# Late modulation columns loaded two ahead, and the last features' products put at the end, in a fused two-block kernel

## The chip, the cores and the metric

The kernel runs on one core of a Trainium2 chip. The metric is the device time of one execution in microseconds (us). A core has TensorE (PE, with its weight loads PEld), VectorE (DVE), ScalarE (ACT), GpSimd (POOL) and SyncE (SP), whose queue issues nearly all DMAs here.

## The reference

Two transformer-like blocks on 256 tokens of 1024 features, in float32. Only block 1 and the end of block 2's mixing touch the change.

```
mod = silu(c) @ w_ada + b_ada            # six vectors of 1024: shift1, scale1, gate1, shift2, scale2, gate2
h   = rmsnorm(x, norm1_g) * (1 + scale1) + shift1
qa, ka, va, qi, ki, wi, qb, kb, vb, ga, gb = split(h @ w_in)
ya  = sparse_attention(qa, ka, va, index scores of qi, ki, wi: the 64 best keys)
yb  = stick_breaking_attention(qb, kb, vb)
m   = sigmoid(ga) * (ya @ w_proj_a) + sigmoid(gb) * (yb @ w_proj_b)
x   = x + gate1 * (m @ w_out)
h2  = rmsnorm(x, norm2_g) * (1 + scale2) + shift2
x   = x + gate2 * experts(h2)            # 16384 experts, the longest part by far
x   = block2(x)                          # SSM and mLSTM branches, mixed @ w_out_2, again experts
```

## The kernel before

Activations stand transposed, features on partitions, 256 tokens along the free side. Every matrix that is streamed comes in column tiles of 128 x 1024 floats (512 KB), one DMA each on SP's queue (`wload`, L200). A tile in `raw` is split in two fp32r parts: `whi` by a cast on ScalarE (L180) and `wlo` = raw - whi on VectorE (L181). The stream has 3 `raw`, 3 `whi` and 2 `wlo` buffers. `flow` (L208) loads one tile ahead of the one that it hands out.

One output tile is 24 products into one PSUM tile (`wstat`, L217): for each of 8 feature groups k, whi·hi and whi·lo, and after these 16 the 8 of wlo·hi. PSUM has four tiles "mm" and four "acc".

Block 1 in order: `w_vab` and `w_qk` together with the first 16 modulation dots; then 30 tiles of `w_in`, numbered 0 to 29 here, through `proj` (L483): 6 for the index vectors, 8 for qa and ka, 16 for the two gates. Between them run generators by budget (`Side.run`): stick-breaking (`stick`), index scores and the choice of keys (`index`), attention (`attend`, which reads `toep`, the table of position biases). Then the mixing stage (L700): 8 tiles of `w_pab`, the products ya·w_proj_a and yb·w_proj_b, gated and added on VectorE (L711 to L713) and split into `mhi`, `mlo`. Then 8 tiles of `w_out` (L723), whose results go into `xT` (L727), into two scaled parts `u` for the queries (`unscaled`, L302) and into a row sum of squares on TensorE (`sq_acc`, L275). `queries` (L309) makes the first 5 query tiles from u, and the reciprocal root of the row sum scales them afterwards.

The late modulation vectors (indices 2, 3 and 4: gate1, shift2, scale2) are 24 dots (`mod_dot`, L343), each the product of a 128 x 1024 piece of `w_mod` with the row `crow`, summed along the row, one VectorE instruction and a short read of the accumulator. Its 512 KB come by a DMA from the same SP queue. `mods_late` (L356) is a generator: a step loads a piece into one of 2 buffers and computes its dot. `proj` gives it 1.3 in each of the first 14 tiles and 0.35 in the rest, the mixing stage 0.8 a tile; a step costs 1.3 and is taken while the sum is positive. `late.finish()` after the mixing stage runs what is left.

What the code says is a program order with priorities. The framework's scheduler orders the instructions of each engine at build time from that, from dependences and from an estimated timeline, so products of two tiles can stand between each other. `issue_after(x)` keeps an instruction behind x on its engine.

Block 2 has the same shape at its end: mixing, 8 tiles of `w_out_2` (L1496) and `queries`.

Of the kernel before, what the change touches and what calls it, by code (L numbers as in the profile page):

```python
# [9 lines left out]
F32 = mybir.dt.float32  # L10
# [11 lines left out]
P = 128  # L22
T = 256
D = 1024
NK = 8
# [84 lines left out]
class K:  # L110
# [106 lines left out]
    def wstat(self, p, w, a, n, k0=0, ks=None, parts=(0, 1), first=True, last=True):  # L217
# [6 lines left out]
        for c, (x, y, k) in enumerate(ops):  # L224
            nc.tensor.matmul(p, x[:, (k0 + k) * P:(k0 + k + 1) * P], y[:, k, :], start=first and c == 0,  # L225
                             stop=last and c == len(ops) - 1)

    def wmove(self, acc, w, a, k, n, t0=0):

        nc = self.nc  # L230
        whi, wlo = w
        ahi, alo = a
        for tt in range(2):
            ts = slice(t0 + tt * P, t0 + (tt + 1) * P)
            for i, (x, y) in enumerate(((ahi, whi), (ahi, wlo), (alo, whi))):
                for h in range(2):
                    nc.tensor.matmul(acc[2 * tt + h], x[:, k, ts], y[:, h * 512:(h + 1) * 512],  # L237
                                     start=k == 0 and i == 0, stop=k == n - 1 and i == 2)
# [70 lines left out]
    def queries(self, flow, u, x, a, b, pss, pool, tags):  # L309


        nc, NU = self.nc, self.NU
        n = T if b is None else T + 2
        room = [self.t(self.const, [P, D], F32, "row", 2).rearrange("p (i t) -> p i t", t=T)
                for _ in range(0, NU, 4)]
        qb = None if b is None else self.t(pool, [P, NU], F32, "qb")
        self.qs = []
        h2 = self.act_pair()
        at = 0
        for i in range(NU):  # L320
            w = next(flow)
            p = self.ps()
            if i == 0:
                self.wstat(p[:, :n], w, u, NK, parts=(0,), last=False)
                self.sq_acc(pool, pss, x[:, NK - 1], NK - 1, tags[0])
                r = self.rstd_t(pool, pss, tags[1])
                self.wstat(p[:, :n], w, u, NK, parts=(1,), first=False)
            else:
                self.wstat(p[:, :n], w, u, NK)
            q = room[i // 4][:, i % 4]  # L330
            nc.vector.tensor_tensor(q, p[:, :T], r, ALU.mult)
            if b is not None:
                nc.scalar.copy(qb[:, i:i + 1], p[:, T:T + 1])
                nc.scalar.activation(q, q, AF.Identity, bias=qb[:, i:i + 1])
            self.qs.append((i, q))
            e = min(NK, 2 * (i + 1))
            self.scaled(pool, x, r, a, b, *h2, tag=tags[2], ks=range(at, e))
            at = e
        self.w0 = next(flow)
        return h2  # L340


    def mod_dot(self, i, k, raw):  # L343

        self.nc.sync.dma_start(raw, self.A["w_mod"][i, k])
        self.nc.vector.scalar_tensor_tensor(raw, raw, 1.0, self.crow, op0=ALU.mult, op1=ALU.mult,
                                            accum_out=self.mods[:, i, k:k + 1])

# [6 lines left out]

    def mods_late(self, pool, parts):  # L356

        for i in parts:
            for k in range(NK):
                raw = self.t(pool, [P, D], F32, "raw", 2)  # L360
                with self.tc.issue_after(self.wdma.ins):
                    self.mod_dot(i, k, raw)
                yield 1.3
            self.mod_end(i, 0, NK, "norm2_g" if i == 4 else None)

    def mod_gate2(self, pool):

# [23 lines left out]
    def block1(self):  # L391
        nc, A, tc = self.nc, self.A, self.tc
        v = nc.vector
        es = ExitStack()
        with es:
            wk = self.sub(es, "b1")
# [5 lines left out]
            for i in range(2):  # L402
                x = self.t(self.const, [P, D], F32, f"x{i}")
# [5 lines left out]
            for i in range(2):  # L409
                p = self.ps("acc")  # L410
# [27 lines left out]
            for k in range(0, NK, 2):  # L438
                p = self.ps()
# [10 lines left out]
            with tc.tile_pool(name="mods", bufs=1, side="right", reuse_waits="tile") as mp:  # L450
                for k in range(NK):
                    for i in (1, 0):
                        self.mod_dot(i, k, self.t(mp, [P, D], F32, "raw", 4))
                    a, b = (self.mods[:, i, k:k + 1] for i in (1, 0))
                    nc.scalar.activation(a, a, AF.Identity, scale=self.col("norm1_g", k), bias=gb[:, k:k + 1])
                    nc.scalar.activation(b, b, AF.Identity, bias=self.col("b_ada", k))
                    w = self.wload(A["w_vab"][k])
                    f = self.t(wk, [P, T], F32, "hnf", 2)
                    nc.scalar.activation(f, xr[:, k], AF.Identity, scale=a, bias=b)
                    self.split(h[0][:, k], h[1][:, k], f)  # L460
                    self.wmove(acc, w, h, k, NK)
                    whi, wlo = self.wload(A["w_qk"][k])
                    for i, (x, y) in enumerate(((whi, h[0]), (whi, h[1]), (wlo, h[0]))):
                        for j in range(8):
                            nc.tensor.matmul(pqk[j // 2][:, j % 2 * T:(j % 2 + 1) * T], x[:, j * P:(j + 1) * P], y[:, k],  # L465
                                             start=k + i + j % 2 == 0, stop=k == NK - 1 and i == 2 and j % 2 == 1,
                                             skip_group_check=True)
# [7 lines left out]
            for i in range(4):  # L475
                nc.scalar.activation(qkb[:, 2 * i:2 * i + 2], pqk[i].rearrange("p (k t) -> p k t", k=2), AF.Copy,
                                     scale=0.125 if i < 2 else 1.0)
            late = Side(self.mods_late(wk, (2, 3, 4)))
            budget = iter([1.3] * 14)
            flow = self.flow(*(A["w_in"][i] for i in range(30)), *(A["w_pab"][i] for i in range(NK)),  # L480
                             *(A["w_out"][i] for i in range(NK)), *(A["wq1"][i] for i in range(self.NU + 1)))

            def proj(dst, n=P, scale=None):  # L483
                w = next(flow)
                p = self.ps()
                self.wstat(p[:, :T], w, h, NK)
                late.run(next(budget, self.bl))
                if scale:
                    nc.scalar.activation(dst, p[:n, :T], AF.Copy, scale=scale)
                else:  # L490
                    nc.scalar.copy(dst, p[:n, :T])
# [183 lines left out]
            for i in range(8):  # L675
                if i < 4:
                    proj(qa[:, i], scale=0.125)
                else:
                    proj(ka[:, i - 4])
                if i % 2 == 0:  # L680
                    with tc.issue_after(self.wdma.ins):
                        nc.sync.dma_start(toep[:, i:i + 2], A["toep"][:, i:i + 2])
                ix.run(2.4)
                side.run(0.8)
            ix.finish()
# [11 lines left out]
            last = self.last  # L697
            mhi = self.t(wk, [P, NK, T], F32R, "qkb")
            mlo = self.t(wk2, [P, NK, T], F32R, "m_lo")
            for c in range(NK):  # L700
                w = next(flow)
                late.run(self.bs)
                pa = self.ps()
                self.wstat(pa[:, :T], w, ya, 4)
                pb = self.ps()
                self.wstat(pb[:, :T], w, yb, 4, k0=4)
                with tc.issue_after(last.ins):
                    last = nc.scalar.activation(sg[:, c:16:8], sg[:, c:16:8], AF.Sigmoid)
                m1 = self.t(wk2, [P, T], F32, "m1", 2)
                m2 = self.t(wk2, [P, T], F32, "m2", 2)  # L710
                nc.vector.tensor_tensor(m1, pa[:, :T], sg[:, c], ALU.mult)  # L711
                nc.vector.tensor_tensor(m2, pb[:, :T], sg[:, 8 + c], ALU.mult)
                nc.vector.tensor_tensor(m1, m1, m2, ALU.add)  # L713
                self.split(mhi[:, c], mlo[:, c], m1)
            self.ln_exp(last)
            late.finish()
            pss = self.ps("acc")
            u = self.t(wk2, [P, 2, NK, T + 2], F32R, "sg")
            u = (u[:, 0], u[:, 1])
            a2, b2 = self.mods[:, 4], self.mods[:, 3]  # L720
            bb = b2.unsqueeze(2).to_broadcast([P, NK, 2])
            self.split(u[0][:, :, T:], u[1][:, :, T:], bb)
            for c in range(NK):  # L723
                w = next(flow)
                p = self.ps()
                self.wstat(p[:, :T], w, (mhi, mlo), NK)
                nc.vector.scalar_tensor_tensor(xT[:, c], p[:, :T], self.mods[:, 2, c:c + 1], xT[:, c],  # L727
                                               op0=ALU.mult, op1=ALU.add)
                self.unscaled(u, xT, a2, c)
                if c < NK - 1:  # L730
                    self.sq_acc(wk, pss, xT[:, c], c)
# [693 lines left out]
    wait, bt = 3, 0.9  # L1425
    NU = 5
    ha, hi = 100, 100
    bl, bs, b5, bm, bf = 0.35, 0.8, 1.3, 1.8, 1.1

    def mix(self, wk, es, xm, M, sz, sgs, sgm, ysg):  # L1430

# [64 lines left out]
        for c in range(NK):  # L1496
            w = next(flow)
            p = self.ps()
            self.wstat(p[:, :T], w, (mx[0][:, :, :T], mx[1][:, :, :T]), NK)
            v.tensor_tensor(x3T[:, c], p[:, :T], x3T[:, c], ALU.add)  # L1500
            self.unscaled(u, x3T, g2, c)
            if c > 0:
                self.sq_acc(wk, pss, x3T[:, c - 1], c - 1, "cs")
# [500 lines left out]
```

## Time and profile before

| | |
|---|---|
| median of three executions | 2151.61 us (2148.75 to 2153.57) |
| profiled execution | 2151.88 us |
| its span, first to last instruction | 2150.2 us |
| TensorE busy | 2116.2 us (98%) |
| VectorE busy | 1615.7 us (75%) |
| ScalarE busy | 1118.5 us (52%) |
| TensorE's mean granted clock | 0.994 |
| DMA, mean over the span | 187 GB/s |

Busy time counts an engine's instructions from start to end. TensorE's instructions overlap one another, so its busy share says when it had something to do, and the granted clock how fast it was allowed to. Times in the trace count from the start of the span.

### The profile page before, as it was taken

How to read it: one execution, taken by the hardware profiler on the slowest of the kernel's cores; microseconds unless marked ns; L12 is line 12 of the kernel's file. 1: busy time of each engine (PE TensorE's matmuls, PEld its weight loads, DVE VectorE, ACT ScalarE, POOL GpSimd, SP SyncE). 2: the span in 40 equal slices, each digit the busy share in tenths (PEclk: the TensorE clock that was granted, in tenths of full speed). 3: DMA queues.
4: the chain of work that ended last, by engine and by line, in shares of the span. 5: the costliest groups of instructions: out<-in, count | busy, mean ns of one | idle time of the engine just before them, and what ended most of it. 6: DMA issues, size and time to landing. Idle time of an engine off the chain costs nothing.

```text
span 2150.2 us, 39275 instructions
## 1 busy us (share of the span) xinstructions
PE 2116.2 (98%) x14926; PEld 1925.0 (90%) x14926; DVE 1615.7 (75%) x3728; ACT 1118.5 (52%) x2157; POOL 20.8 (1%) x71
## 2 busy tenths in 40 slices
PE   8999999999999999999999999999999999999998
PEld 7889999999999887777788989999999998888886
DVE  8687799778889698666566457899688896555565
ACT  6546555455444554555464565455555445445553
POOL 0100000000000000000000000000000000000000
PEclk9999999999999999999999999999999999999999
DMA  9755556655555777767666525566555556666664
GB/s 333 248 191 180 177 170 195 186 167 161 164 164 162 249 227 238 203 202 205 197 187 191 184 79 157 181 183 196 167 158 165 161 166 187 194 196 192 192 193 138
DMA packets 127472, 402.44 MB, mean 187 GB/s; under 512 B 19617, under 2 KB 31521, under 8 KB 127026
## 3 DMA queue, kind: packets, MB, share of 16 engines
q1 hardware_dynamic: 127282, 399.93, 60.9%
q8 instruction: 117, 1.92, 0.4%
q14 instruction: 73, 0.60, 0.1%
HBM read 389.75 MB, written 9.03 MB: 185 GB/s over the span
## 4 chain that ended last, share of the span: by engine, by line
PE 90%; DMA 4%; DVE 3%; ACT 2%; issue 1%; POOL 0%; SPq 0%; DVEq 0%; ACTq 0%; POOLq 0%
PE ps_mm L225 47%; PE ps_acc L1126 31%; PE ps_acc L1015 1%; PE ps_acc L1016 1%; DVE wlo L181 1%; ACT whi L180 1%; PE ps_acc L237 1%; PE ps_mm L465 1%; DMA raw<-in_wq 1%; DMA raw<-in_v 1%; DMA raw<-in_w_in 1%; PE ps_acc L878 1%; PE ps_mm L243 1%; PE ps_mm L1367 1%; PE ps_acc L1662 0%
## 5 line engine op out<-in xcount | busy, mean ns | idle before, releaser
L180 ACT CAST whi<-raw 128x1024 fp32r<-128x1024 f32 x628 | 660.5, 1052 | 788.7 <-PE ps_acc L1126 279.4
L181 DVE TENSOR_TENSOR wlo<-raw,whi 128x1024 fp32r<-128x1024 f32 x521 | 637.0, 1223 | 319.4 <-ACT whi L180 180.9
L225 PE MATMUL ps_mm<-act_hi,whi 128*128 128x256 f32 (+1 forms) x2608 | 651.2, 288 | 3.7 <-ACT whi L180 1.2
L225 PE MATMUL ps_mm<-act_lo,whi 128*128 128x256 f32 (+1 forms) x2608 | 637.7, 283 | 0.0
L225 PEld LDWEIGHTS ps_mm<-act_hi,whi 128*128 128x128 f32 x2608 | 490.4, 189 | 9.7 <-issue 3.4
L225 PEld LDWEIGHTS ps_mm<-act_lo,whi 128*128 128x128 f32 x2608 | 492.2, 189 | 2.6 <-issue 1.9
L225 PE MATMUL ps_mm<-act_hi,wlo 128*128 128x256 f32 (+1 forms) x2544 | 354.8, 281 | 0.0
L225 PEld LDWEIGHTS ps_mm<-act_hi,wlo 128*128 128x128 f32 x2544 | 324.5, 189 | 1.4 <-issue 1.0
L181 DVE TENSOR_TENSOR xwlo<-raw,whi 128x1024 fp32r<-128x1024 f32 x107 | 130.8, 1222 | 82.8 <-ACT whi L180 81.4
L1126 PE MATMUL ps_acc<-whi,gh 128*128 128x512 f32 x328 | 103.4, 396 | 0.1
L1126 PE MATMUL ps_acc<-whi,gl 128*128 128x512 f32 x328 | 103.2, 396 | 0.1
L1126 PE MATMUL ps_acc<-whi,clo 128*128 128x512 f32 x328 | 102.6, 394 | 0.1
L1126 PE MATMUL ps_acc<-wlo,I1T 128*128 128x512 f32 x328 | 100.9, 390 | 0.0
L1126 PE MATMUL ps_acc<-whi,chi 128*128 128x512 f32 x328 | 89.0, 390 | 0.8 <-ACT chi L180 0.8
L1126 PE MATMUL ps_acc<-whi,I2T 128*128 128x512 f32 x328 | 88.5, 390 | 0.8 <-ACT I2T L180 0.8
L1126 PE MATMUL ps_acc<-whi,I1T 128*128 128x512 f32 x328 | 88.5, 390 | 0.0
L1126 PEld LDWEIGHTS ps_acc<-whi,chi 128*128 128x128 f32 x328 | 61.5, 188 | 14.1 <-ACT chi L180 1.2
L1126 PEld LDWEIGHTS ps_acc<-whi,I2T 128*128 128x128 f32 x328 | 61.4, 188 | 14.0 <-ACT I2T L180 1.2
L1126 PEld LDWEIGHTS ps_acc<-whi,gh 128*128 128x128 f32 x328 | 60.3, 188 | 14.6 <-issue 2.0
L1126 PEld LDWEIGHTS ps_acc<-wlo,I1T 128*128 128x128 f32 x328 | 61.6, 188 | 13.1
L1126 PEld LDWEIGHTS ps_acc<-whi,I1T 128*128 128x128 f32 x328 | 61.3, 188 | 13.0 <-ACT I1T L180 0.3
L1126 PEld LDWEIGHTS ps_acc<-whi,clo 128*128 128x128 f32 x328 | 60.6, 188 | 13.8 <-issue 1.2
(585 smaller groups left out, 3383.3 us busy)
## 6 DMA issues: line engine op xcount, KB each, us to landing
raw<-in_u SPq DMA_DIRECT2D x256, 512.0 KB, 3.7
raw<-in_v SPq DMA_DIRECT2D x256, 512.0 KB, 4.3
raw<-in_w_in SPq DMA_DIRECT2D x66, 512.0 KB, 4.3
raw<-in_w_mod SPq DMA_DIRECT2D x40, 512.0 KB, 5.3
raw<-in_wq SPq DMA_DIRECT2D x32, 512.0 KB, 3.8
raw<-in_w_out SPq DMA_DIRECT2D x16, 512.0 KB, 3.7
raw<-in_w_vab SPq DMA_DIRECT2D x8, 512.0 KB, 5.3
raw<-in_w_qk SPq DMA_DIRECT2D x8, 512.0 KB, 5.3
```

The source lines that it names most:

```text
L180: nc.scalar.copy(hi, src)
L181: nc.vector.tensor_tensor(lo, src, hi.bitcast(F32), ALU.subtract)
L225: nc.tensor.matmul(p, x[:, (k0 + k) * P:(k0 + k + 1) * P], y[:, k, :], start=first and c == 0, stop=last and c == len(ops) - 1)
L237: nc.tensor.matmul(acc[2 * tt + h], x[:, k, ts], y[:, h * 512:(h + 1) * 512], start=k == 0 and i == 0, stop=k == n - 1 and i == 2)
L243: self.nc.tensor.transpose(out, in_, self.ident[b:b + n, b:b + n])
L465: nc.tensor.matmul(pqk[j // 2][:, j % 2 * T:(j % 2 + 1) * T], x[:, j * P:(j + 1) * P], y[:, k], start=k + i + j % 2 == 0, stop=k == NK - 1 ...
L878: nc.tensor.matmul(p2[:, tt * P:(tt + 1) * P], q[:, tt * P:(tt + 1) * P], keys[:, hc // 8, (hc % 8) * P:(hc % 8 + 1) * P], start=tt == 0, ...
L1015: nc.tensor.matmul(o, oa[:, i], ob[:, i], start=i == 0, stop=False, skip_group_check=True)
L1016: nc.tensor.matmul(o, oa[:, i], oc[:, i], start=False, stop=i == 3, skip_group_check=True)
L1126: nc.tensor.matmul(acc[2 * tt + lo // 512][:, lo % 512:(hi - 1) % 512 + 1], x[:, ts], y[:, lo:hi], start=i == 0 and q == 0, stop=i == P - ...
L1367: nc.tensor.matmul(p[:64, i * P:(i + 1) * P], bbz[:, r, i].rearrange("p e c -> p (e c)"), ca[:, r, i, 0:8].rearrange("p l c -> p (l c)"), ...
```

## The change

The late dots get three buffers, and a step first issues the loads of the pieces up to two ahead, then computes its own dot. Their order becomes 2, 4, 3. The budget is 1.3 in the first 6 w_in tiles, 0.65 in the next 8 and 0.57 in the last 16; the mixing stage has none, and the first 7 w_out tiles have 1.3 each, the eighth what is left. The columns that carry shift2 into the queries are written in the eighth w_out tile. The four loads of `toep` move from w_in tiles 6, 8, 10 and 12 to 10, 11, 12 and 13. `wlast` gives one tile's products in the order of the features: both parts of groups 0 to 6, then both parts of group 7. The first `w_out` tile, the first `w_out_2` tile and the first query tile use it; in the query tile the last row sum stands between the two and the reciprocal root behind both.

```diff
+    def wlast(self, p, w, a, between=None):
+
+        self.wstat(p, w, a, NK, ks=range(NK - 1), last=False)
+        if between:
+            between()
+        self.wstat(p, w, a, NK, ks=(NK - 1,), first=False)
+
...
             if i == 0:
-                self.wstat(p[:, :n], w, u, NK, parts=(0,), last=False)
-                self.sq_acc(pool, pss, x[:, NK - 1], NK - 1, tags[0])
+                self.wlast(p[:, :n], w, u, lambda: self.sq_acc(pool, pss, x[:, NK - 1], NK - 1, tags[0]))
                 r = self.rstd_t(pool, pss, tags[1])
-                self.wstat(p[:, :n], w, u, NK, parts=(1,), first=False)
...
     def mod_dot(self, i, k, raw):
 
-        self.nc.sync.dma_start(raw, self.A["w_mod"][i, k])
...
-        for i in parts:
-            for k in range(NK):
-                raw = self.t(pool, [P, D], F32, "raw", 2)
+        todo = [(i, k) for i in parts for k in range(NK)]
+        raws = []
+        for n, (i, k) in enumerate(todo):
+            for j in range(len(raws), min(n + 3, len(todo))):
+                raws.append(self.t(pool, [P, D], F32, "raw", 3))
                 with self.tc.issue_after(self.wdma.ins):
-                    self.mod_dot(i, k, raw)
-                yield 1.3
-            self.mod_end(i, 0, NK, "norm2_g" if i == 4 else None)
+                    self.nc.sync.dma_start(raws[j], self.A["w_mod"][todo[j]])
+            self.mod_dot(i, k, raws[n])
+            yield 1.3
+            if k == NK - 1:
+                self.mod_end(i, 0, NK, "norm2_g" if i == 4 else None)
...
-            late = Side(self.mods_late(wk, (2, 3, 4)))
-            budget = iter([1.3] * 14)
+            late = Side(self.mods_late(wk, (2, 4, 3)))
+
+            budget = iter([1.3] * 6 + [0.65] * 8 + [0.57] * 16)
...
-                late.run(next(budget, self.bl))
+                late.run(next(budget))
...
-                if i % 2 == 0:
+                if i > 3:
                     with tc.issue_after(self.wdma.ins):
-                        nc.sync.dma_start(toep[:, i:i + 2], A["toep"][:, i:i + 2])
+                        nc.sync.dma_start(toep[:, 2 * i - 8:2 * i - 6], A["toep"][:, 2 * i - 8:2 * i - 6])
...
             for c in range(NK):
                 w = next(flow)
-                late.run(self.bs)
                 pa = self.ps()
...
-            late.finish()
...
-            self.split(u[0][:, :, T:], u[1][:, :, T:], bb)
             for c in range(NK):
                 w = next(flow)
+                if c < NK - 1:
+                    late.run(1.3)
+                else:
+                    late.finish()
+                    self.split(u[0][:, :, T:], u[1][:, :, T:], bb)
                 p = self.ps()
-                self.wstat(p[:, :T], w, (mhi, mlo), NK)
+                if c == 0:
+                    self.wlast(p[:, :T], w, (mhi, mlo))
+                else:
+                    self.wstat(p[:, :T], w, (mhi, mlo), NK)
...
-            self.wstat(p[:, :T], w, (mx[0][:, :, :T], mx[1][:, :, :T]), NK)
+            mix = (mx[0][:, :, :T], mx[1][:, :, :T])
+            if c == 0:
+                self.wlast(p[:, :T], w, mix)
+            else:
+                self.wstat(p[:, :T], w, mix, NK)
```

## Rows read from the trace of the kernel before

**Rows 1.** The page, busy time, share of the span and instructions of each engine.

```profile
PE 2116.2 (98%) x14926; PEld 1925.0 (90%) x14926; DVE 1615.7 (75%) x3728; ACT 1118.5 (52%) x2157; POOL 20.8 (1%) x71
```

**Rows 2.** Windows: length, busy PE, PEld, DVE, ACT, POOL, clock, DMA share, GB/s.

```profile
62.00:82.00 20.00, 20.00 (x163) 18.59 (x162) 13.23 (x20) 10.39 (x18) 2.52 (x4) 1.00 0.86 307
82.00:110.00 28.00, 24.36 (x135) 18.96 (x135) 18.90 (x36) 12.52 (x30) 5.71 (x8) 0.82 0.50 185
110.00:143.00 33.00, 32.67 (x244) 28.77 (x244) 29.45 (x80) 14.68 (x30) 2.60 (x6) 1.00 0.50 161
143.00:197.00 54.00, 52.53 (x413) 47.22 (x412) 39.07 (x82) 34.63 (x77) 1.46 (x2) 1.00 0.56 188
197.00:224.00 27.00, 24.24 (x194) 23.13 (x194) 23.99 (x43) 14.54 (x21) 0.00 (x0) 1.00 0.73 262
224.00:228.00 4.00, 4.00 (x22) 4.00 (x22) 3.86 (x11) 1.96 (x4) 0.00 (x0) 0.57 0.46 137
228.00:252.00 24.00, 24.00 (x194) 23.68 (x193) 15.21 (x25) 13.43 (x23) 0.00 (x0) 1.00 0.53 154
```

**Rows 3.** Waits of TensorE, 197 to 300: total us, times, longest.

```profile
PE ps_mm L225 <- DVE m L711: 2.6, 1, 2.6
PE ps_mm L225 <- ACT qb L333: 0.6, 1, 0.6
```

**Rows 4.** Windows of L346 alone (busy DVE, two instructions a dot), clock, DMA, GB/s.

```profile
197.00:228.00 31.00, 6.14 (x10) 0.94 0.70 246
```

**Rows 5.** Waits of TensorE, 62 to 110.

```profile
PE ps_mm L586 <- ACT relu L592: 2.6, 2, 1.4
PE ps_acc L533 <- POOL sp L528: 1.1, 1, 1.1
```

**Rows 6.** Waits of VectorE, 62 to 110.

```profile
DVE raw L346 <- DMA raw<-in_w_mod: 9.4, 8, 2.4
```

**Rows 7.** Timeline of VectorE: start, duration, instruction, idle time before it.

```profile
82.17 1.23 DVE L346 SCALAR_TENSOR_TENSOR raw<-raw,crow 128x1024 f32<-128x1024 f32 x1 [2.43 <-DMA raw<-in_w_mod]
83.33 0.08 DVE L346 DVE_READ_ACCUMULATOR raw<-raw,crow 128x1 f32 x1
```

**Rows 8.** Timeline of SP's issues.

```profile
77.55 0.42 SPq L345 DMA_DIRECT2D raw<-in_w_mod  x1
78.01 0.43 SPq L682 DMA_DIRECT2D toep<-in_toep  x1
86.92 0.33 SPq L204 DMA_DIRECT2D raw<-in_w_in  x1
...
90.60 0.33 SPq L204 DMA_DIRECT2D raw<-in_w_in  x1
...
97.28 0.33 SPq L345 DMA_DIRECT2D raw<-in_w_mod  x1
```

**Rows 9.** Timeline of ScalarE.

```profile
94.80 1.04 ACT L180 CAST whi<-raw 128x1024 fp32r<-128x1024 f32 x1 [2.38 <-DMA raw<-in_w_in]
```

**Rows 10.** Groups of VectorE, 197 to 226: count, busy us, mean ns, idle before.

```profile
L181 DVE TENSOR_TENSOR wlo<-raw,whi 128x1024 fp32r<-128x1024 f32 x9 | 10.9, 1219 | 0.3 <-ACT whi L180 0.3
...
L711 DVE TENSOR_TENSOR m<-ps_mm,sg 128x256 f32<-128x256 f32 x7 | 2.9, 418 | 0.5 <-PE ps_mm L225 0.5
```

**Rows 11.** Timeline of TensorE in w_out.

```profile
237.63 0.59 PE L279 MATMUL ps_acc<-sq,ones 128*128 128x256 f32 x2
...
238.18 1.12 PE L225 MATMUL ps_mm<-qkb,wlo 128*128 128x256 f32 x8
239.14 0.28 PE L225 MATMUL ps_mm<-qkb,whi 128*128 128x256 f32 x1
```

**Rows 12.** Groups of VectorE, 228 to 252.

```profile
L727 DVE SCALAR_TENSOR_TENSOR xT<-ps_mm,mods,xT 128x256 f32<-128x256 f32 x7 | 3.4, 483 | 7.2 <-PE ps_mm L225 7.2
L306 DVE SCALAR_TENSOR_TENSOR sg<-xT,mods,sg 128x256 fp32r<-128x256 f32 x7 | 3.3, 481 | 0.4 <-ACT sg L305 0.4
```

**Rows 13.** The page, DMA issues: KB each, median us from issue to landing.

```profile
raw<-in_w_mod SPq DMA_DIRECT2D x40, 512.0 KB, 5.3
```

More of the change, by code (lines that the diff above doesn't have):

```diff
@@ L452, in block1 @@
                     for i in (1, 0):
-                        self.mod_dot(i, k, self.t(mp, [P, D], F32, "raw", 4))
+                        raw = self.t(mp, [P, D], F32, "raw", 4)
+                        nc.sync.dma_start(raw, A["w_mod"][i, k])
+                        self.mod_dot(i, k, raw)
                     a, b = (self.mods[:, i, k:k + 1] for i in (1, 0))
@@ L1427 @@
     ha, hi = 100, 100
-    bl, bs, b5, bm, bf = 0.35, 0.8, 1.3, 1.8, 1.1
+    b5, bm, bf = 1.3, 1.8, 1.1
     def mix(self, wk, es, xm, M, sz, sgs, sgm, ysg):
```

## The prediction

> **What bounds the kernel now.** I read the page first. TensorE is busy for 98% of the span and no other engine comes near it [rows 1], so a change in block 1 can only pay where TensorE stands idle or runs at its half clock. The view by windows shows where that is in the stretches that this change touches [rows 2]. Three stretches have neither idle time nor a low clock (62 to 82, 228 to 252) or almost none (110 to 143). Two are poor:
>
> - 82 to 110 (w_in tiles 8 to 12, stick-breaking and index work between them): busy 24.36 of 28.00 us, so 3.64 idle, at a granted clock of 0.82. The clock has two levels, 2.4 and 1.2 GHz; a mean of 0.82 is 0.36 of 28 us = 10.1 us at the lower one, in which half the work is lost: 5.0 us. Together 8.7 us.
> - 197 to 228 (mixing stage, start of w_out): 2.76 us idle in 197 to 224, then a clock of 0.57 over 4.00 us, 1.7 us lost. Together 4.5 us.
>
> 143 to 197 adds 1.47 us of idle time. So what this change can reach in block 1 is about 8.7 + 4.5 + 1.5 = 14.7 us.
>
> Then I asked who is late. In 197 to 228 it is one wait of 2.6 us: the next product needs a PSUM tile that VectorE (L711) has not read yet [rows 3]. VectorE is busy 23.99 of 27.00 us there [rows 2], of which 6.1 us are five modulation dots at L346 [rows 4]; the sixth of that region stands ahead of 197. VectorE is the bound of the mixing stage, TensorE should be next.
>
> In 82 to 110 the waits are small ones on ScalarE's relu and GpSimd's mask [rows 5], and the cause lies further back. VectorE waited 9.4 us in 62 to 110 for w_mod loads, eight times [rows 6]. Its queue is in order: the dot at 82.17 came 2.43 us late [rows 7], and behind it stood the stick work and the weight splits that free stream buffers. So SP, whose last issues were at 77.55 and 78.01, loaded no weights until 86.92 [rows 8]. Then everything started at once: four w_in, four w_mod and two toep loads from 86.92 to 97.28. The w_in load of 90.60 was the one ScalarE waited for until 94.80 (2.38 us idle) [rows 8, 9], the relu of the index work stood behind that cast, TensorE idled, and its clock fell.
>
> **The change, part by part.** All in microseconds against the profiled execution, 2151.88 (span 2150.2 and 1.7 around it; 0.3 above the median of 2151.61).
>
> *How many dots go where.* From the budgets, one dot costing 1.3 and a step taken while the debt is positive. Before: 14 in tiles 0 to 13, 4 in tiles 14 to 29, 6 in the mixing stage or at its end. After: 6 in tiles 0 to 5, 4 in tiles 6 to 13, 8 in tiles 14 to 29, none in the mixing stage, 6 in the first six w_out tiles. The number of dots by then is the same, 18. Loads run two ahead: 12 instead of 14 by tile 13, and 4 fall into w_out.
>
> *Mixing stage.* Six dots of 1.22 leave it (7.3). Per tile VectorE then has one split at 1.22 and four operations at 0.42 (L711 and three like it), 2.9 as durations [rows 10], and less on the clock, since each overlaps the next (the dot of 82.17 took 1.23, its successor started 1.16 later [rows 7]). TensorE has 24 products at 0.12 = 2.9 (eight from 238.18 to 239.14 [rows 11]). The 2.8 of idle time and the 1.7 of clock both go: **-4.5**. Bounds 0 (if another chain takes the wait) and -4.5.
>
> *Tiles 6 to 13.* Four dots instead of eight, no dot waits for its own load, and the first toep pair moves from tile 6 to tile 10, the others to 11, 12 and 13. In the burst of 86.92 to 97.28, two w_mod and one or two toep loads go away, some 1.6 of 5.0 MB. The 2.43 wait at the head of the chain goes. What is late next is the chain VectorE, ScalarE, GpSimd, TensorE of the stick work itself. I take somewhat over half of 8.7: **-5.0**. Bounds 0 and -8.7.
>
> *Tiles 14 to 29.* Four dots more (4.9 on VectorE, which goes from 39.07 to 44 of 54 busy), four loads more (2.1 MB on 188 GB/s over 54 us, 227). VectorE in 110 to 143, at 29.45 of 33, gets lighter, and the late weight of 143 to 149 with it. **-0.5**; bounds -1.5 and +1.5, the idle time of that stretch gone or doubled.
>
> *w_out, first six tiles.* VectorE has a split, xT and the low half per tile, 1.22 + 0.48 + 0.48 [rows 10, 12], and now a dot: 3.4 as durations, some 3.1 as they overlap. TensorE has 2.9 of products and 0.4 of the fp32 row sum (237.63 to 238.18, less one product [rows 11]), 3.3. VectorE goes from 15.21 to about 22.5 of 24 [rows 2]. What hides the dots is that margin of 0.2 a tile, and it is thin. **+1.0**; bounds 0 and +3 (about the one wait of 2.6 that a full VectorE cost in the mixing stage [rows 3]).
>
> *First step.* Three w_mod loads stand ahead of w_in tile 2, where one did. Two more 0.5 MB loads at 307 GB/s are 3.4 us for that one weight. TensorE has no idle time in 62 to 82 to show how near the weights are; the two tiles that are already loaded (5.7 us of products) hide it. **0**; bound +1.7 if only half is hidden.
>
> *Last features last* (the first w_out tile, the first w_out_2 tile, and the first query tile, whose code both blocks run). Feature 7 is needed after 21 products instead of 14, that is 0.8 later. But the waits of TensorE have none at any of them (the longest in 197 to 300 are those of [rows 3]): the build's scheduler already puts the second tile's products between those of the first. So nothing to gain, bound -0.2. In the query tile the row sum now comes after 21 instead of 16 products, so the reciprocal root is up to 0.6 later; TensorE waits 0.6 for a query copy (L333) in block 1 [rows 3], which can grow. **+0.3**; bounds 0 and +1.2, 0.6 in each block.
>
> Sum: -4.5 - 5.0 - 0.5 + 1.0 + 0 + 0.3 = -8.7, so 2151.9 - 8.7 = **2143.2**.
>
> The idle rows and the clock rows were added above since TensorE's busy time alone would show 3.64 lost in 82 to 110. The Trainium skill (Perfetto Trace Analysis, Identifying the Most-Contended Engine) says that matmul occupancy misleads and that the busy share of weight loads is the better measure. By it 82 to 110 has lost 28.00 - 18.96 = 9.0, which agrees with the 8.7 [rows 2]; but 110 to 143 and 143 to 197 would then have lost 4.2 and 6.8 where the idle rows show 0.3 and 1.5. That reading is the first rival.
>
> **The rivals.**
>
> *More comes back.* Weight loads leave 11.0 unfilled in 110 to 197 [rows 2]. If steadier weights filled half of it, 5.5 more: 2137.7. Against it: TensorE hardly waits there, and the index and attention products are small or fp32 and leave the loader idle by their form. 0.05.
>
> *Only the mixing stage gains.* The early stretch may stay as it is: its waits end on relu and on GpSimd [rows 5], and the scheduler orders all engines anew at build. Then -4.5 - 0.5 + 1.0 + 0.3 = -3.7: 2148.2. For it: the same amount of w_mod by tile 13 less two. Against: the 2.43 wait ahead of the empty load queue. 0.15.
>
> *The mixing stall moves to w_out.* VectorE at its limit there gives back 4.5 where I have 1.0 in mind: -8.7 + 3.5 + 1.0 for a product that waits for a split = -4.2: 2147.7. 0.13.
>
> *Slower: dots in w_out wait for their loads.* This is one mechanism, at VectorE's queue in the first six w_out tiles. A dot that waits there as the longest did (2.4 [rows 6]) holds up xT and the splits: six times 2.4, and 0.6 (3.4 against 3.3 a tile), less a tile in hand of 3.3 = 11.7 idle, and a clock fall like that of 82 to 110, 5.0: 16.7 on the -9.7 that the sum has without w_out, 2158.9. It makes the kernel slower by over 4.3 from a wait of (9.7 + 4.3 - 5.0 + 3.3 - 0.6) / 6 = 2.0 a dot on. Against it: a load is issued two tiles, 6.6, ahead, and lands in 5.3 [rows 13]. For it: the load two ahead takes the buffer that the dot one step back has just read, and SP's queue is in order, so a late dot also holds up the weight loads queued behind that load. 0.15.
>
> **How the numbers follow.** The forecast has 0.52, with a range of its own from 2137 to 2147. Below 2137 only part of the first rival lies. 0.2% of 2151.6 is 4.3, about what a measurement of this kernel can tell from no change: faster is under 2147.3. Faster gets the forecast, the first rival and a third of the second and third: 0.52 + 0.05 + 0.05 + 0.04 = 0.66. Slower gets most of the last, 0.13, the rest is 0.21. The range goes from 2137 (-8.7 - 4.5 - 1.5 at its lower bounds) to 2153, and leaves out some 0.13 above and under 0.05 below.
>
> **What would show it.** Right: waits of L346 on w_mod near zero; no wait on L711 and a clock of 1.00 in the mixing stage; SP issuing w_in with no 9 us gap around w_in tile 8; a clock over 0.9 in the stretch that answers to 82 to 110; VectorE near 90% in w_out with TensorE idle for under 1 us. Wrong: the early stretch with its low clock still there, in which case the sum loses 5.0; VectorE idle ahead of L346 in w_out; a new low-clock stretch anywhere in the first 270 us.

## The result, and the profile after

The changed kernel takes 2138.84 us (median of six executions, 2136.67 to 2142.61) against 2151.60 (six, 2146.89 to 2153.57): a ratio of 0.9945, interval 0.993 to 0.996. That is 12.8 us less where 8.4 to 8.7 were forecast; it is inside the range, near its lower end. The profiled execution of after took 2136.67, the shortest of the six, and its span fell by 15.2 us, from 2150.2 to 2135.0.

TensorE's row of the page of after, to be held against [rows 1]: its busy time fell by 7.9 us with the same count of products. The mean granted clock rose from 0.994 to 0.997, about 6.5 us of 2135, so most of that is time no longer spent at the lower clock.

```profile
PE 2108.3 (99%) x14926; PEld 1919.6 (90%) x14926; DVE 1615.4 (76%) x3728; ACT 1119.0 (52%) x2157; POOL 21.7 (1%) x71
```

The windows of after, cut at about the same work as [rows 2] (which stands 9 us earlier now at the mixing stage and over 13 at the end of w_out); columns as there:

```profile
61.00:81.00 20.00, 20.00 (x162) 18.59 (x160) 16.44 (x25) 12.54 (x20) 4.91 (x4) 1.00 0.94 363
81.00:101.00 20.00, 19.80 (x143) 16.51 (x144) 16.17 (x31) 12.92 (x31) 2.99 (x7) 1.00 0.51 178
101.00:134.00 33.00, 32.44 (x251) 28.95 (x250) 30.00 (x84) 14.80 (x31) 5.32 (x9) 1.00 0.47 156
134.00:188.00 54.00, 53.07 (x415) 47.60 (x415) 41.37 (x83) 35.92 (x79) 0.00 (x0) 1.00 0.66 222
188.00:212.00 24.00, 24.00 (x200) 23.53 (x200) 19.34 (x36) 13.18 (x19) 0.00 (x0) 1.00 0.62 195
212.00:216.00 4.00, 4.00 (x36) 4.00 (x35) 4.00 (x10) 1.05 (x1) 0.00 (x0) 1.00 1.00 359
216.00:239.00 23.00, 22.00 (x174) 21.40 (x173) 17.40 (x32) 13.32 (x24) 0.00 (x0) 1.00 0.61 193
```

I read them with one sum that is used from here on: what TensorE lost in a window is its idle time (length less busy PE) plus length times (1 - clock), half the time spent at 1.2 GHz.

- Early stretch, w_in tiles 8 to 12: 0.2 lost in 81 to 101, against 3.64 + 5.04 = 8.7 in [rows 2].
- The rest of w_in, 101 to 188: 0.56 + 0.93 = 1.5, against 0.33 + 1.47 = 1.8.
- Mixing stage, 188 to 212: nothing, against 4.5.
- w_out, 212 to 239: 1.0, against nothing.

That makes 8.5 + 0.3 + 4.5 - 1.0 = 12.3. Behind the first five query tiles of block 2, where the products read the scaled features (`act_hi`), the kernel before has a wait of 1.0 at 1357.05 that was not among the rows ahead. This is its row in the waits of TensorE, 1320 to 1380, kernel before:

```profile
PE ps_mm L225 <- ACT act_hi L180: 1.0, 1, 1.0
```

The same stretch of after, 1310 to 1370, has no wait of TensorE at all. This brings the sum to 13.3; the other 1.9 of the 15.2 lies in pieces under 1 us that I don't trace. The start of the w_in stage is none of them: its first load is issued at 52.73 before and at 52.89 after.

Where the wait went, in the waits of TensorE of after, 188 to 290, beside [rows 3]:

```profile
PE ps_mm L225 <- DVE m_lo L181: 1.0, 1, 1.0
PE ps_mm L225 <- ACT act_hi L305: 0.4, 1, 0.4
```

And why, in VectorE's timeline of after at the start of w_out:

```profile
217.70 1.23 DVE L350 SCALAR_TENSOR_TENSOR raw<-raw,crow 128x1024 f32<-128x1024 f32 x1 [1.32 <-DMA raw<-in_w_mod]
218.85 0.08 DVE L350 DVE_READ_ACCUMULATOR raw<-raw,crow 128x1 f32 x1
218.85 0.42 DVE L181 TENSOR_TENSOR m_lo<-m,qkb 128x256 fp32r<-128x256 f32 x1
```

The dot at 217.70 stood 1.32 us for its load, and the low half of the last mixing feature, which the first w_out tile needs, stood behind it.

The dots did not go where the budgets put them. These are the windows of after with the dot's line alone (VectorE's busy time, two instructions a dot):

```profile
61.00:81.00 20.00, 9.83 (x16) 1.00 0.94 363
81.00:101.00 20.00, 3.70 (x6) 1.00 0.51 178
101.00:134.00 33.00, 2.46 (x4) 1.00 0.47 156
134.00:188.00 54.00, 8.62 (x14) 1.00 0.66 222
188.00:212.00 24.00, 0.79 (x1) 1.00 0.62 195
212.00:239.00 27.00, 4.11 (x8) 1.00 0.67 217
```

20 dots are done by 188 and four stand in w_out (the first begins at 211.21); the prediction had 18 and six. The budgets give the program order; the build's scheduler moved two dots ahead of it.

### The profile page after: what moved, and what is told of

Read it like the earlier page. It is cut to its first block, busy times and chain, and to the rows that moved or that the text cites. A ratio compares the mean times of both kernels' runs of the same rounds, so it can differ in the third digit from the quotient of the medians.

```text
span 2135.0 us, 39269 instructions
## 1 busy us (share of the span) xinstructions
PE 2108.3 (99%) x14926; PEld 1919.6 (90%) x14926; DVE 1615.4 (76%) x3728; ACT 1119.0 (52%) x2157; POOL 21.7 (1%) x71
## 4 chain that ended last, share of the span: by engine, by line
PE 93%; DVE 3%; DMA 2%; ACT 1%; issue 0%; SPq 0%; DVEq 0%; ACTq 0%
PE ps_mm L225 49%; PE ps_acc L1142 32%; PE ps_acc L1031 1%; PE ps_acc L1032 1%; PE ps_acc L244 1%; PE ps_mm L475 1%; DVE wlo L181 1%; ACT whi L180 1%; PE ps_acc L894 1%; PE ps_mm L250 1%; DMA raw<-in_v 1%; PE ps_mm L1383 1%; PE ps_acc L1682 0%; PE ps_acc L1706 0%; PE ps_acc L1627 0%
## 5 line engine op out<-in xcount | busy, mean ns | idle before, releaser
L1142 PE MATMUL ps_acc<-whi,I1T 128*128 128x512 f32 x328 | 88.5, 390 | 0.0
L1142 PEld LDWEIGHTS ps_acc<-wlo,I1T 128*128 128x128 f32 x328 | 61.6, 188 | 13.2
```

The costliest lines, as they stand in the source:

```text
L1142: nc.tensor.matmul(acc[2 * tt + lo // 512][:, lo % 512:(hi - 1) % 512 + 1], x[:, ts], y[:, lo:hi], start=i == 0 and q == 0, stop=i == P - ...
```

## Experiments

Each was timed in five rounds against the kernel before on the same chip. The median of the kernel before was 2151.61 in the rounds of e1 to e4, 2150.14 in those of e5 to e8 and 2151.26 in those of e9 to e12, so kernels of different rounds are better compared by their ratios. "Lost" is the sum defined above, from the windows of one profiled execution of each kernel, which need not be a typical one: those of after, e1, e5 and e11 were the shortest of theirs, that of e3 the longest of eleven.

| | median us | ratio [interval] | lost early | lost in mixing | lost in w_out |
|---|---|---|---|---|---|
| before | 2151.6 | | 8.7 | 4.5 | 0 |
| after | 2138.84 | 0.9945 [0.993, 0.996] | 0.2 | 0 | 1.0 |
| e1: loads two ahead alone | 2143.14 | 0.9964 [0.995, 0.9977] | 0.2 | 3.6 | 0 |
| e2: places of the dots alone | 2146.84 | 0.9981 [0.997, 0.9991] | 3.4 | 0 | 1.7 |
| e3: places of toep alone | 2148.92 | 0.9984 [0.9975, 0.9992] | 7.6 | 1.8 | 0.3 |
| e4: last features alone | 2150.30 | 0.9993 [0.9984, 1.0001] | 6.5 | 3.4 | 1.4 |
| e5: after, own loads | 2143.33 | 0.997 [0.9958, 0.9982] | 0.5 | 0 | 2.5 |
| e6: after, dots in the mixing stage | 2142.16 | 0.9958 [0.9944, 0.9972] | 0.2 | 2.6 | 1.4 |
| e7: after, old product order | 2144.93 | 0.9973 [0.9961, 0.9985] | 0.3 | 0 | 1.9 |
| e8: after, no dot in w_out tile 0 | 2139.89 | 0.9948 [0.9935, 0.9962] | 0.3 | 0 | 1.6 |
| e9: before, dots that wait for no load | 2154.08 | 1.0012 [1.0, 1.0024] | 4.5 | 0 | 0 |
| e10: after, old places of toep | 2139.77 | 0.9952 [0.9938, 0.9965] | 0.2 | 0 | 3.5 |
| e11: after, last feature last in two tiles | 2139.37 | 0.9948 [0.9934, 0.9961] | 0.3 | 0 | 1.4 |
| e12: after, unaltered | 2139.61 | 0.9945 [0.9933, 0.9958] | 0.2 | 0 | 3.7 |

### One part alone: e1 to e4

e1 gives the kernel before three buffers and issues up to two loads ahead, the budgets of the dots staying as they were:

```diff
+        for n, (i, k) in enumerate(todo):
+            for j in range(len(raws), min(n + 3, len(todo))):
+                raws.append(self.t(pool, [P, D], F32, "raw", 3))
...
+                    self.nc.sync.dma_start(raws[j], self.A["w_mod"][todo[j]])
+            self.mod_dot(i, k, raws[n])
```

> The kernel before, with the late loads issued two dots ahead into three buffers and nothing else changed (places of the dots, toep and the order of products as before). Theory A (two separate stalls: late loads make the early one, too many dots the mixing one): the waits of L346 fall from 11.8 us to under 4, the early stretch gains 3 to 9, the mixing stage keeps its 2.6 us wait: -3 to -9 us. Rival B (all is the waits for w_mod): -11 to -14 us, the mixing stall goes too. Rival C (any edit reorders the engines, and the early stall with its low clock goes with the order): about -9 here and as much in the toep-only and products-only kernels.

e2 has the new budgets and the order 2, 4, 3, but each dot issues its own load into two buffers:

```diff
-            budget = iter([1.3] * 14)
+            budget = iter([1.3] * 6 + [0.65] * 8 + [0.57] * 16)
...
-                late.run(self.bs)
...
+                if c < NK - 1:
+                    late.run(1.3)
```

> The kernel before, with the dots in the places of the changed kernel (budgets, order 2, 4, 3, none in the mixing stage, the last six in w_out), each still loaded by its own step into two buffers. Theory A: the mixing stage gains its 4.5 us, the early stretch at most half of its 9 since dots still wait for their loads, w_out loses 1 to 3 to such waits: -4 to -8 us. Rival B: 0 to -2 us. Rival C: about -9 in the early stretch and -4.5 in mixing, -13.

e3 moves the toep loads, e4 adds `wlast` in its three places, each with the lines of the change's own diff and nothing else.

> The kernel before with the four toep loads moved to the ka tiles and nothing else. Theory A: two 0.4 MB loads leave the burst of w_in tiles 8 to 11: 0 to -2 us. Rival C: the early stall goes or moves with the new order, -5 to -9 us or as much the other way.

> The kernel before with the three output tiles' products in the order of the features and nothing else. Theory A and rival B: within 1 us of before (no wait at these tiles). A second theory of the end of block 2, where 1.2 us came back behind the queries: it is this edit, and shows here as -1.2 us behind the first block-2 query product. Rival C: as for the toep-only kernel, a change of several us in the first 250 us though nothing there was late for these products.

The window of the early stretch in e1, where it is shorter:

```profile
82.00:101.00 19.00, 18.84 (x139) 15.81 (x139) 16.66 (x32) 12.27 (x30) 3.21 (x6) 1.00 0.72 265
```

The same stretch in e2:

```profile
84.00:112.00 28.00, 26.27 (x164) 20.36 (x163) 19.94 (x39) 17.07 (x43) 6.00 (x9) 0.94 0.39 142
```

In e3:

```profile
84.00:112.00 28.00, 25.40 (x140) 19.48 (x139) 19.38 (x38) 14.15 (x36) 6.97 (x9) 0.82 0.44 165
```

And in e4:

```profile
83.00:111.00 28.00, 24.89 (x147) 19.33 (x143) 20.49 (x39) 13.96 (x35) 4.93 (x8) 0.88 0.48 181
```

In these executions loads two ahead alone win the whole early stretch; the new places of the dots win over half of it, those of toep and the product order little. The mixing stage is the reverse: e2 loses nothing there, and e1 still has a wait, in the waits of TensorE (185 to 300, e1):

```profile
PE ps_mm L225 <- DVE m L717: 1.9, 1, 1.9
```

But it is not the stall of the kernel before. VectorE is busy for only 22.13 us of e1's 29.00 there, with three dots, and the `m` that TensorE waits for stands behind a dot that waits for its load, as VectorE's timeline of e1 shows:

```profile
202.55 1.23 DVE L345 SCALAR_TENSOR_TENSOR raw<-raw,crow 128x1024 f32<-128x1024 f32 x1 [1.33 <-DMA raw<-in_w_mod]
...
204.03 0.42 DVE L717 TENSOR_TENSOR m<-ps_mm,sg 128x256 f32<-128x256 f32 x1
```

The four gains in the median are 8.5 + 4.8 + 2.7 + 1.3 = 17.3, more than the 12.8 together; that e1 and e2 win part of the early stretch twice would account for it, and the 1.3 of e4 is not told from nothing. Against what was expected: the totals of e1 and e2 lie in their ranges, but the waits of e1's dots fell to 6.6 in all and not under 4, and e2 won more than half of the early stretch; e3 gained more than the 2 us at most.

### What in "two ahead" clears the early stretch: e5, e9, e10

The prediction's chain was: a dot waits for its load, stick-breaking and weight splits wait behind it, SP finds no free stream buffer for 9 us, then everything is loaded at once. e5 is the changed kernel with each dot loading its own piece again:

```diff
-            for j in range(len(raws), min(n + 3, len(todo))):
-                raws.append(self.t(pool, [P, D], F32, "raw", 3))
+            for j in range(len(raws), min(n + 1, len(todo))):
+                raws.append(self.t(pool, [P, D], F32, "raw", 2))
```

> The changed kernel with two buffers and each dot loaded by its own step again, places kept. Theory A (loads ahead make the early gain, places the mixing gain): the early stretch loses most of its 9 us again, 5 to 8, the mixing stage keeps its gain; -4 to -8 us against before. Rival (once the dots are fewer in tiles 6 to 13, loads ahead add nothing): within 2 us of the changed kernel, -10 to -13.

e9 is the kernel before, whose late dots read `crow` alone, so that none waits for a load:

```diff
+        self.nc.sync.dma_start(raw, self.A["w_mod"][i, k])
+        junk = self.t(pool, [P, D], F32, "junk", 1)
+        self.nc.vector.scalar_tensor_tensor(junk, self.crow, 1.0, self.crow, op0=ALU.mult, op1=ALU.mult,
```

> The kernel before, in which the 24 late dots multiply crow with itself instead of the piece of w_mod that was loaded (mods 2 to 4 come out wrong); all loads stay where they were, so the bytes and SP's queue are the same, and only VectorE's wait for each load is gone. Theory (VectorE's wait for a load just issued starves the stream in the early stretch): the first product of the mixing stage comes at 187 to 189 us instead of 196.4, no low clock between 90 and 115, and the time is 8 to 10 us under before, 2141 to 2143, as with loads two ahead (2143.14); the dots still stand in the mixing stage, so its wait stays. Rival (it is the load queue, by bytes and order, not VectorE's wait): the low clock near 98 stays and the time is within 3 us of before.

e10 puts the toep loads of the changed kernel back to `if i % 2 == 0`.

> The changed kernel with the toep loads back at w_in tiles 4, 6, 8 and 10. Theory (the early stretch is won by the loads two ahead alone, which gave all of it with the old places): the same time as the changed kernel within 2 us, 2137 to 2141, and no low clock between 90 and 115. Rival (the later toep loads carry their own share, as e3 alone gave 0.16%): 3 to 4 us above the changed kernel, 2142 to 2143.

e9 can't be read by its total. It is 2.8 us slower than the kernel before. The scheduler drew the free dots forward, 14 of the 24 into the first 65 us, where ScalarE waited 13.3 us for w_vab loads (1.6 in the kernel before), and SP issued the first w_in load at 64.75 instead of 52.73. No dot is left behind 94, so the mixing stage has none either, against what was expected, and loses nothing. Behind that start it has lost 4.5 instead of 8.7 in the stretch that answers to 82 to 110. This is the window of e9 for all engines:

```profile
94.00:122.00 28.00, 26.85 (x157) 20.57 (x154) 15.48 (x29) 15.83 (x38) 6.08 (x9) 0.88 0.48 179
```

And here for the dot's line alone:

```profile
0.00:65.00 65.00, 16.44 (x27) 0.92 0.80 274
...
94.00:122.00 28.00, 0.00 (x0) 0.88 0.48 179
```

SP's timeline in e9 still has the gap, 8.3 us from the end of a toep issue to the next w_in:

```profile
89.50 0.42 SPq L689 DMA_DIRECT2D toep<-in_toep  x1
98.19 0.33 SPq L204 DMA_DIRECT2D raw<-in_w_in  x1
```

So neither the dot nor its wait is needed for the gap. Where the dot of 82.17 stood before, VectorE now waits for TensorE's product of the stick work:

```profile
94.60 1.02 DVE L529 TENSOR_SCALAR sp<-ps_acc 128x384 uint32<-128x384 uint32 x2 [4.48 <-PE ps_acc L524]
```

What goes with a shorter gap stands in ScalarE's timeline. In after, two weight casts are ahead of the stick-breaking instruction that waits for VectorE:

```profile
77.97 1.04 ACT L180 CAST whi<-raw 128x1024 fp32r<-128x1024 f32 x1
79.86 1.04 ACT L180 CAST whi<-raw 128x1024 fp32r<-128x1024 f32 x1 [0.85 <-DMA raw<-in_w_in]
81.31 0.52 ACT L535 ACTIVATE sp<-sp 128x384 f32<-128x384 f32 x1 [0.41 <-DVE sp L533]
```

In e5, as in before, e2, e3, e4 and e9, there is one, and the next cast stands behind the whole stick work:

```profile
76.95 1.05 ACT L180 CAST whi<-raw 128x1024 fp32r<-128x1024 f32 x1 [1.23 <-DVE wlo L181]
...
83.40 0.53 ACT L535 ACTIVATE sp<-sp 128x384 f32<-128x384 f32 x1 [4.50 <-DVE sp L533]
...
86.17 1.05 ACT L180 CAST whi<-raw 128x1024 fp32r<-128x1024 f32 x1 [0.47 <-PE ps_mm L225]
```

VectorE's splits follow the casts, and SP's w_in issues follow the splits. SP's timeline of after has a gap of 6.2 us (76.40 + 0.42 to 82.98), of e1 5.6 (77.80 + 0.42 to 83.82). In after:

```profile
76.40 0.42 SPq L368 DMA_DIRECT2D raw<-in_w_mod  x1
82.98 5.84 SPq L204 DMA_DIRECT2D raw<-in_w_in  x2
```

The last row merges two issues. A timeline from 84 on shows the second by itself:

```profile
88.50 0.33 SPq L204 DMA_DIRECT2D raw<-in_w_in  x1
```

So SP stands again from 83.3 to 88.5: loads two ahead did not close the gap, they put one weight load into it. In e1 the same load stands at 83.82 and the next at 89.33.

And in e5, where the gap is 8.6:

```profile
77.36 0.42 SPq L368 DMA_DIRECT2D raw<-in_w_mod  x1
86.39 2.45 SPq L204 DMA_DIRECT2D raw<-in_w_in  x2
88.89 0.42 SPq L368 DMA_DIRECT2D raw<-in_w_mod  x1
90.24 2.15 SPq L204 DMA_DIRECT2D raw<-in_w_in  x2
92.44 0.42 SPq L368 DMA_DIRECT2D raw<-in_w_mod  x1
92.92 0.42 SPq L693 DMA_DIRECT2D toep<-in_toep  x1
```

Yet e5's profiled execution loses only 0.5 early, with dots that wait 6.1 us in 50 to 112. Of the kernels with the long gap it has the fewest other loads among and right behind the four w_in loads that follow: two w_mod and one toep. Counting the loads of the burst in SP's timeline in the same way: e2 two and two, 3.4 lost; e3 four and one, 7.6; e4 and before four and two, 6.5 and 8.7. e9 also has four and two and loses 4.5 without the dots, and e1, whose gap is split, has four and two and loses 0.2. So a weight load inside the gap goes with no loss under a heavy burst (e1) and a light one (after, two and one); that a lighter burst helps behind a long gap fits the rows, but no run changed the burst alone.

And e5's profiled execution is no typical one: with 2137.72 us at a mean granted clock of 0.997 it was the shortest of six; the others took 2141.22 to 2147.82 at 0.994 or 0.995, about the clock of the kernel before (0.993 to 0.995), and where they lost it no trace shows. By the median e5 is 6.8 us under the kernel before, as the theory expected, and the loads two ahead are worth some 4 us in the changed kernel, though the two intervals still touch.

In e10 the toep loads are back, a weight load stands in the gap (at 82.85), and next to nothing (0.2) is lost early: toep's places earn nothing that can be measured once the loads are two ahead (2139.77 against e12's 2139.61).

That the build's order for the engines, and not the dot's wait, makes the gap is read from these timelines and not shown; no run changed that order alone. Why the scheduler chose it with loads two ahead stays open.

### Dots in the mixing stage and in w_out: e6, e8, e11, e12

e6 gives the changed kernel 0.35 instead of 0.57 in the last 16 w_in tiles and `late.run(0.8)` in each mixing tile again. e8 starts the w_out dots at tile 1:

```diff
-                if c < NK - 1:
+                if 0 < c < NK - 1:
                     late.run(1.3)
-                else:
+                elif c:
```

e11 uses `wlast` for `c < 2`; e12 is the changed kernel itself, timed in the same rounds as e9 to e11.

> The changed kernel with the gate tiles' budget at 0.35 and 0.8 in the mixing stage as before, so some dots stand in the mixing stage again, now with loads ahead (the rest in w_out as after). Theory A (VectorE's time bounds the mixing stage, not its waits for loads): the wait on L711 comes back, the stage is 2 to 4 us longer, -8 to -10 us against before. Rival (the mixing stall was late loads): no wait, -12 us.

> The changed kernel with the six w_out dots in tiles 1 to 6 instead of 0 to 5. The one wait left at the start of w_out is 1.0 us on m_lo, behind a dot that waited 1.32 us for its load. If the dots cause it, it goes: -13 us against before, 1 better than the changed kernel. If not, it stays, or the dots crowd the last w_out tiles ahead of the queries: -10 to -12.

> The changed kernel with the last feature's products last in the first two w_out tiles, not in the first alone. In the changed kernel TensorE waits once at the start of w_out, 1.0 us for the low half of a mixing feature. Theory (that wait belongs to the last feature's split, which two tiles of other products cover and one does not): the wait goes and the time is about 1 us lower, 2137 to 2139, which these rounds can hardly tell from no change; its trace tells it. Rival (the split itself is late, behind a dot): the wait stays as it is.

> The changed kernel unaltered, on the chip of the three runs before it. Nothing should differ: 2137 to 2142, ratio 0.993 to 0.996. If it comes out above 2143, differences of 3 to 4 us between variants of the changed kernel are no evidence.

e6 brings the stall back without any wait of the dots to speak of (0.5 in all, 180 to 217). Its window of the mixing stage:

```profile
187.00:216.00 29.00, 26.36 (x212) 25.20 (x211) 25.67 (x46) 14.75 (x22) 0.00 (x0) 1.00 0.81 292
```

Its row in the waits of TensorE:

```profile
PE ps_mm L225 <- DVE m L722: 4.1, 2, 2.6
```

VectorE is busy 25.67 of 29.00 there, and it is the bound of this stage by its work. The second of the two waits, 1.4, ends at 218.91, behind that window, and makes the 1.4 of e6's last column. The dots there cost 2.6 to 3.3 us in the median (against the 2139.61 and 2138.84 of the unaltered kernel), though the intervals of the ratios overlap; 8.0 under the kernel before is what the theory expected.

e12 shows that w_out differs between executions of one and the same kernel. Its window:

```profile
212.00:241.00 29.00, 27.01 (x205) 26.48 (x204) 21.33 (x39) 14.70 (x25) 0.00 (x0) 0.94 0.62 201
```

And its wait of TensorE there:

```profile
PE ps_mm L225 <- DVE m_lo L181: 2.0, 1, 2.0
```

The dot of after's 217.70 waits 1.91 there instead of 1.32, TensorE 2.0 instead of 1.0, and the clock falls once: 3.7 lost instead of 1.0. Moving the first dot (e8) or covering more (e11) doesn't help. In e8 the scheduler again puts a dot ahead of the last `m_lo`, which waits 1.88 for its load, and TensorE waits 1.6; its median is 10.3 under the kernel before, as expected where the wait stays. In e11 the wait is 0.7 for `m_lo` and 0.7 for a weight cast, which is neither of the two outcomes expected. Neither time differs from e12's, so no version here beats the changed kernel.

### The product order in the changed kernel: e7

e7 takes `wlast` out of all three places.

> The changed kernel with the old order of products in the three output tiles. If the 1.2 us behind block 2's queries are this edit, they are lost here, and the wait on the last mixing column at the first w_out tile grows by up to 0.8: -10 to -11 us against before. If the edit does nothing: -12.

It is slower than after by 2144.93 - 2138.84 = 6.1 us, and the intervals of the two ratios do not meet, though the same edit alone on the kernel before (e4) stays inside what can be measured. Neither expectation holds: it is 5.2 under the kernel before in its rounds, not 10 to 12. Of the 6.1 its trace shows about 2: in w_out 1.9 lost instead of 1.0, and in the waits of TensorE this row behind block 1's first five query tiles, where the products read `act_hi`:

```profile
PE ps_mm L225 <- ACT act_hi L305: 1.1, 1, 1.1
```

And this one at the same place of block 2:

```profile
PE ps_mm L225 <- ACT act_hi L180: 0.6, 1, 0.6
```

The second is in none of the eight kernels with `wlast` (after, e4 to e6, e8, e10 to e12) and in all six without it (0.5 to 1.1). The first is 0.2 to 0.5 in six of the eight and not there in e4 and e5; without `wlast` it is 0.9 (e1, e2), 1.1 (e7), 0.4 (e9) or not there (before, e3). How the order at the first query tile shortens a wait behind the fifth is not shown. The rest of the 6.1 stays open, and not all of it lies at the edited tiles: in the first 30 us TensorE stands idle for 9.57 us in e7 and for 8.14 and 8.45 in the two executions of the changed kernel, with this row in the waits of e7 (0 to 62), which is 0.3 and 0.7 in those:

```profile
PE ps_acc L445 <- DVE ss L442: 1.8, 1, 1.8
```

## Why the prediction came out right, and where its steps did not

**The place of the gain** was right: 13 of the 15.2 us of span lie in the two poor stretches named from [rows 2]. The size was not: 12.8 in the median, half as much again as forecast. 2138.84 even lies nearer to the 2137.7 of the rival *more comes back* than to the 2143.2, but what that rival named was not seen (below).

**Mixing stage**, -4.5: measured 4.5 lost before and nothing after. e2 and e9 show that a stage without dots has no wait, e6 that putting them back brings it back. VectorE as the bound, read from [rows 2, 3], holds, though in e1 a dot's wait for its load brings a wait with VectorE far from full. The count was off by one: by the budgets the kernel before has five dots in tiles 14 to 29 and five in the mixing stage, not four and six, and its trace has five there [rows 4].

**Tiles 6 to 13**, -5.0: this is the term that was mis-sized. I took somewhat over half of 8.7, since I expected the stick work's own chain to be late next; 8.5 came back. That is 3.5 more than the term, over half of the 6.5 by which the profiled pair (15.2) went beyond the sum of 8.7; the wait that went behind block 2's first five query tiles makes 1.3 more (-1.0 where the term for the last features was +0.3), and 1.9 is not traced. The reason given was also only part of it. The 2.43 us wait [rows 7] was blamed for the gap of [rows 8]; in e9 the gap outlives the dots, and what is late there is the stick work's product, the chain that I expected next. In e1 and after a weight load stands inside the gap, which the prediction did not foresee. That the burst behind the gap costs time fits the rows and is not shown by itself. One reading of the burst was wrong: the load that ScalarE awaited until 94.80 is that of 88.51, which landed 6.2 us after its issue, and not that of 90.60, which landed at 98.2; the chain stays the same.

**Waits of the dots near zero**: wrong. In 50 to 260 VectorE still waits 7.6 us for w_mod, ten times, up to 1.7 (11.8, twelve times, in all of the kernel before), as its waits in after say:

```profile
DVE raw L350 <- DMA raw<-in_w_mod: 7.6, 10, 1.7
```

**w_out**, +1.0 with bounds 0 and +3: 1.0 in after, 3.7 in e12 with its low clock, so the upper bound was short by the clock. That the 1.0 was met is luck. It came neither from six dots nor from VectorE at 90% (21.40 of 27.00 in 212 to 239, 79%), but from one dot that waited ahead of one split. The rival "dots in w_out wait for their loads" has its mechanism here, once instead of six times, and far from the 2.0 us on every dot at which it would have decided.

**Last features**, +0.3: the wrong sign, and outside its bounds. That TensorE's waits show none at these tiles was true, but a wait behind them, the 1.0 at 1357.05, stood in the trace and entered no term; with the new order it is gone. How much of e7's 6.1 us belongs to the order stays open.

**More comes back** from 110 to 197 by fuller weight loads: not seen. Weight loads leave 4.05 + 6.40 = 10.5 unfilled in 101 to 188, against 11.0, while TensorE stands idle 1.5 there. The Trainium skill (Perfetto Trace Analysis, Identifying the Most-Contended Engine) has, beside the share of peak work, the busy share of weight loads as the better measure of TensorE; in this stretch the measurement goes with the idle and clock rows instead.

## What to carry to other kernels

Sum idle time and low clock by stretch first: it told where this change could pay, and 13.0 of the 13.2 in the two poor stretches came back. When a queue runs dry, look at the order of the instructions on the engines behind it, not only at the longest wait in front of it: in e9 that wait was taken away and the gap stayed. A scheduler that reorders at build can make a small edit change that order in places that it does not name. A trace is one execution: read its time and clock beside those of the others (e5). And test the parts both ways, alone on the kernel before and taken out of the kernel after: the product order was worth 0.07% by the first, which is not told from nothing, and up to 0.28% by the second.

## What was unexpected of the hardware

A wait of TensorE does not decide by its length whether the granted clock falls. At the start of w_out a wait of 2.4 us (e5) left it at 1.00, and with waits of 1.8 and 2.0 (e10, e12) the stage came to 0.94; in the mixing stage 4.1 us in two waits (e6) left it at 1.00, where after one of 1.9 (e1) the stage came to 0.94. The same kernel, profiled twice, had a fall in w_out once (e12) and not the other time (after).
